# Masked softmax: the masks of the last two batches are moved among the divides on VectorE

## Chip, cores and metric

One core of a Trainium2 chip. The metric is the device time of the kernel in microseconds. The profile's times count from the start of its span, which is about 1.6 us shorter than the device time (155.0 against 156.66 in the profiled execution of the kernel before).

## The reference

```python
batch, heads, seq_q, seq_k = 16, 8, 256, 256
for b in range(batch):
    length = lengths[b]                      # 128 to 255, drawn per batch
    masked = x[b, :, :, :length].copy()
    masked = masked - np.max(masked, axis=-1, keepdims=True)
    exp_masked = np.exp(masked)
    result[b, :, :, :length] = exp_masked / np.sum(exp_masked, axis=-1, keepdims=True)
# the rest of result is 0
```

A batch is 2048 rows of 256 float32, 2 MiB. Batches 0 to 3 are loaded whole; the later loads fetch only a rounded-up prefix of each row. Stores always write whole rows.

## The kernel before

VectorE masks a batch (`clip`: a minimum with a ramp that is hugely negative past the length), ScalarE takes the exponentials with their row sums half a batch at a time, VectorE divides half a batch at a time, and SyncE stores. GpSimd issues the loads from batch 4 on. Batch b sits in slot b % 8; each of the 128 partitions holds `nt` = 16 of its rows (`half` is 8, `quarter` 4), and `ahead` is 4. Cuts are marked.

```python
def parts(b):                       # the pieces in which batch b is stored
    if b == 0:
        cuts = [0, nt]
    elif b < 8:
        cuts = [0, half, half + quarter, nt]
    elif b < 13 or b == batch - 1:
        cuts = [0, half, nt]
    else:
        cuts = [0, nt]              # 13 and 14: whole
    return [slice(i, j) for i, j in zip(cuts, cuts[1:])]
# ... (cut)
# SyncE
for b in range(batch):
    s_b = s_st[b % 2]
    for s in parts(b):
        nc.sync.wait_ge(s_out, 2 * b + (s.stop - 1) // half + 1)      # L117: the divides
        if b >= 2 and s.start == 0:
            nc.sync.wait_ge(s_b, 64 * (b // 2 + 1))                   # L119: store b-2 landed
        nc.sync.dma_start(out=out_f[b, :, s, :], in_=xt[:, b % slots, s, :]
                          ).then_inc(s_b, 16 * ((s.stop - s.start) // quarter))   # L120
for par in range(2):
    nc.sync.wait_ge(s_st[par], 64 * (batch // 2 + 1))                 # L124: all stores landed
# ... (cut)
# VectorE
def divide(b, h):
    s = slice(h * half, (h + 1) * half)
    nc.vector.wait_ge(s_exp, 2 * b + h + 1)
    step(nc.vector.reciprocal(out=inv_sum[:, b, s], in_=row_sum[:, b, s]))        # L221
    nc.vector.wait_ge(s_v, v)
    t = xt[:, b % slots, s, :]
    nc.vector.tensor_tensor(out=t, in0=t,
        in1=inv_sum[:, b, s, None].to_broadcast([P, half, seq_k]), op=ALU.mult
    ).then_inc(s_out, 1)                                                          # L224

mask(0, slice(0, half))
mask(0, slice(half, nt))
for b in range(batch):
    first = b == 0 or b >= ahead
    if first:
        divide(b, 0)
    if b + 1 < batch:
        mask(b + 1, slice(0, nt))
    if not first:
        divide(b, 0)
    divide(b, 1)
# ScalarE waits for s_min (the masks) and counts s_exp up by one for each half batch
```

The softmax here doesn't subtract the row's maximum and nothing guards it: scores larger than these inputs give would overflow.

## Time and profile before

| | kernel before |
|---|---|
| device time, median of 3 | 156.42 us (156.28 to 156.44) |
| VectorE, ScalarE busy | 75%, 68% of the span |
| traffic | 62.08 MB, mean 401 GB/s |
| load of batch 15 lands | 134.97 us |
| store of batch 14 issued | 141.10 us |
| last divide ends | 147.94 us |
| last packet of the last store | 152.99 us |

The last row is from the trace's single packet records: each store comes with sixteen records of 4 bytes, which I take for the ends of the parts of the 16 transfer engines, and I use the start of the last of these. The records don't name the engine.

Two of the page's rows of groups give VectorE's durations. Columns: line, engine, operation, operands and count; then busy us and the mean ns of one; then idle us ahead of them and what ended it.

```profile
L224 DVE TENSOR_TENSOR xt<-xt,inv_sum 128x2048 f32<-128x2048 f32 x32 | 73.3, 2292 | 1.1
L197 DVE SCALAR_TENSOR_TENSOR xt<-down,len_s,xt 128x2048 f32<-128x2048 f32 (+1 forms) x17 | 37.8, 2223 | 14.3 <-DMA xt<-in_x_dram 14.2
```

A multiply takes 2.29 us; the mask's mean of 2.22 mixes in two half-size ones of 1.28, a whole one takes 2.35.

### The profile page before, as it was taken

The numbers are of one execution on the slowest core, as the hardware profiler recorded it, in microseconds if no ns is written. First come the engines' busy times: TensorE is split into PE (matmuls) and PEld (weight loads), VectorE is DVE, ScalarE is ACT, GpSimd is POOL, SyncE is SP. The second block draws the span as 40 slices with busy tenths as digits, with TensorE's granted clock in tenths as the row PEclk, the third lists the DMA queues.
The fourth block names the chain that finished last, engine by engine and source line by source line (L and its number), as shares of the span: only waits on it lengthen the run. The fifth ranks groups of instructions, "written<-read, shape, count | busy, mean of one in ns | idle before, by whom it ended". The sixth has DMA issues, their size and how long they took to land.

```text
span 155.0 us, 1317 instructions
## 1 busy us (share of the span) xinstructions
PE 0.2 (0%) x1; PEld 0.1 (0%) x1; DVE 115.8 (75%) x84; ACT 105.2 (68%) x514; POOL 19.0 (12%) x25
## 2 busy tenths in 40 slices
PE   0000000000000000000000000000000000000000
PEld 0000000000000000000000000000000000000000
DVE  1339999953999696969889696969669619696810
ACT  3097799992692959688795939596973933959500
POOL 4910031000220200200211020202001000000000
DMA  4999999999999999999999999999999999999992
GB/s 110 427 457 410 440 376 422 401 408 440 412 409 392 403 410 420 409 415 414 407 422 406 419 405 411 415 412 424 410 420 412 428 439 427 412 450 423 395 425 85
DMA packets 9988, 62.08 MB, mean 401 GB/s; under 512 B 850, under 2 KB 946, under 8 KB 6274
## 3 DMA queue, kind: packets, MB, share of 16 engines
q1 hardware_dynamic: 5904, 41.95, 65.8%
q0 software_dynamic: 4080, 20.12, 32.0%
q14 instruction: 2, 0.02, 0.0%
q10 hardware_dynamic: 2, 0.00, 0.0%
HBM read 28.51 MB, written 33.55 MB: 400 GB/s over the span
## 4 chain that ended last, share of the span: by engine, by line
DMA 74%; DVE 6%; issue 6%; ACT 4%; POOLq 2%; SPq 1%; ACTq 1%; DVEq 0%
DMA xt<-in_x_dram 65%; DMA out_dram<-xt 10%; ACT xt L254 4%; DVE xt L197 3%; DVE xt L224 3%; ACTq L254 1%; SPq L109 1%; POOLq L132 0%; POOLq L137 0%; SPq L120 0%; POOLq L99 0%; DVE inv_sum L221 0%; SPq L111 0%; POOLq L159 0%; POOLq L155 0%
## 5 line engine op out<-in xcount | busy, mean ns | idle before, releaser
L254 ACT ACTIVATE xt<-xt x256 | 102.4, 402 | 38.6 <-DVE xt L197 38.6
L224 DVE TENSOR_TENSOR xt<-xt,inv_sum 128x2048 f32<-128x2048 f32 x32 | 73.3, 2292 | 1.1
L197 DVE SCALAR_TENSOR_TENSOR xt<-down,len_s,xt 128x2048 f32<-128x2048 f32 (+1 forms) x17 | 37.8, 2223 | 14.3 <-DMA xt<-in_x_dram 14.2
L254 ACT ACTIVATION_READ_ACCUMULATOR xt<-xt x256 | 48.1, 188 | 0.0
L132 POOL DMA_DIRECT2D xt<-in_x_dram x12 | 12.8, 1064 | 96.8 <-issue 57.4
L221 DVE RECIPROCAL inv_sum<-row_sum 128x8 f32<-128x8 f32 x32 | 6.4, 199 | 14.4 <-ACT xt L254 14.4
L151 POOL MEMSET xt<- 128x1536 f32 x4 | 5.3, 1387 | 1.1 <-DVE len_s L188 1.1
L246 ACT ACT_TABLE_LOAD x1 | 1.3, 1283 | 1.6 <-SPq L79 1.6
L180 DVE TENSOR_SCALAR down<-iota_i 128x256 f32<-128x256 int32 x1 | 0.3, 298 | 1.6 <-POOL iota_i L143 1.6
L185 DVE CAST len_b<-word 1x16 bf16<-1x16 int32 x1 | 0.2, 161 | 0.4 <-DMA word<-in_lengths_dram 0.4
L188 DVE TENSOR_SCALAR len_s<-len_f 128x16 f32<-128x16 f32 x1 | 0.2, 174 | 0.3 <-PE len_f L167 0.3
L143 POOL IOTA iota_i<- 128x256 int32 x1 | 0.3, 331 | 0.6 <-SPq L79 0.6
L148 POOL MEMSET seed<- 1x1 f32 x2 | 0.3, 162 | 0.0
L246 ACT ACTIVATE warm<-const-float32-0.0 128x1 f32<-128x1 f32 x1 | 0.2, 203 | 0.0
L146 POOL MEMSET ones<- 1x128 bf16 x1 | 0.2, 196 | 0.0
L167 PE MATMUL len_f<-len_b,ones 1*128 1x16 bf16 x1 | 0.2, 164 | 2.6 <-DVE len_b L185 2.6
L272 POOL MEMSET const-float32-0.0<- 128x1 f32 x1 | 0.1, 99 | 0.3 <-issue 0.3
L167 PEld LDWEIGHTS len_f<-len_b,ones 1*128 1x128 bf16 x1 | 0.1, 99 | 2.6 <-POOL ones L146 2.6
L272 POOL MEMSET const-float32-1.0<- 128x1 f32 x1 | 0.1, 99 | 0.0
L272 POOL MEMSET const-bfloat16-1.0<- 128x1 bf16 x1 | 0.1, 99 | 0.0
L272 POOL MEMSET const-uint8-127<- 128x1 uint8 x1 | 0.1, 99 | 0.0
L272 POOL BASE_LOAD x1 | 0.0, 17 | 0.1
## 6 DMA issues: line engine op xcount, KB each, us to landing
out_dram<-xt SPq DMA_DIRECT2D x19, 1024.0 KB
out_dram<-xt SPq DMA_DIRECT2D x14, 512.0 KB
xt<-in_x_dram SPq DMA_DIRECT2D x3, 2048.0 KB, 16.0
out_dram<-xt SPq DMA_DIRECT2D x3, 2048.0 KB
xt<-in_x_dram POOLq DMA_DIRECT2D x3, 1728.0 KB, 17.8
xt<-in_x_dram POOLq DMA_DIRECT2D x2, 2048.0 KB, 18.5
xt<-in_x_dram POOLq DMA_DIRECT2D x2, 1600.0 KB, 17.3
xt<-in_x_dram POOLq DMA_DIRECT2D x2, 1280.0 KB, 15.0
```

Of the source, the lines that this page charges most:

```text
L109: nc.sync.dma_start(out=xt[:, 0, s], in_=x_f[0, :, s]).then_inc(s_ld[h], 16)
L132: nc.gpsimd.dma_start(out=xt[:, slot, :, :w], in_=x_n[:, n, :, :w]).then_inc(s_sw[par], 16)
L143: nc.gpsimd.iota(iota_i, pattern=[[1, seq_k]], base=0, channel_multiplier=0).then_inc(s_iota, 1)
L148: nc.gpsimd.memset(seed[:, par : par + 1], 0.0).then_inc(s_st[par], 64)
L151: nc.gpsimd.memset(xt[:, b, :, low:], 0.0).then_inc(s_fill, 1)
L167: nc.tensor.matmul(len_f, lhsT=ones, rhs=len_b, start=True, stop=True).then_inc(s_lenf, 1)
L197: return nc.vector.scalar_tensor_tensor(out=t, in0=down[:, None, lo:hi].to_broadcast([P, s.stop - s.start, hi - lo]), scalar=len_s[:, b : ...
L221: step(nc.vector.reciprocal(out=inv_sum[:, b, s], in_=row_sum[:, b, s]))
L224: nc.vector.tensor_tensor(out=t, in0=t, in1=inv_sum[:, b, s, None].to_broadcast([P, half, seq_k]), op=ALU.mult,).then_inc(s_out, 1)
L246: nc.scalar.activation(out=warm, in_=nc.const_aps.tensor(0.0, (P, 1), F32), func=EXP)
L254: ins = nc.scalar.activation(out=e, in_=e, func=EXP, accum_out=sum_h[:, bass.ds(i, 1), j])
L272: nc = _bacc.Bacc("TRN2", target_bir_lowering=False, num_devices=1)
```

## The change

The intent is to have VectorE do in the last stretch what is ready: the divides of batch 13 need not stand behind the wait for batch 14's load, and the last mask, which starts the last exponentials, goes as early as it can.

```diff
-            first = b == 0 or b >= ahead
-            if first:
-                divide(b, 0)
-            if b + 1 < batch:
-                mask(b + 1, slice(0, nt))
-            if not first:
-                divide(b, 0)
-            divide(b, 1)
+            at = 0 if b == batch - 2 else 2 if b == batch - 3 else 1 if b == 0 or b >= ahead else 0
+            for h in range(3):
+                if h == at and b + 1 < batch:
+                    mask(b + 1, slice(0, nt))
+                if h < 2:
+                    divide(b, h)
```

`at` is the number of a batch's two divides that go ahead of the next batch's mask: now both for batch 13 and none for batch 14. For all other batches the order is the same as before.

## The prediction

> **What bounds the kernel now.** I read the page's forty slices first. The row of transfer engines stands at 9 from the second slice to the last but one, and the rate stays at 375 to 457 GB/s; VectorE is busy 75% and ScalarE 68% of the span.
>
> ```profile
> DMA  4999999999999999999999999999999999999992
> GB/s 110 427 457 410 440 376 422 401 408 440 412 409 392 403 410 420 409 415 414 407 422 406 419 405 411 415 412 424 410 420 412 428 439 427 412 450 423 395 425 85
> ```
>
> So the kernel is bound by its traffic (62.08 MB), and a reordering on VectorE can gain only where it fills a hole in that row, and can lose only where it makes one. The page's chain agrees in the large, but it needs care at its end:
>
> ```profile
> DMA 74%; DVE 6%; issue 6%; ACT 4%; POOLq 2%; SPq 1%; ACTq 1%; DVEq 0%
> ```
>
> It is followed back from the last compute instruction, not from the last byte. The last compute instruction is the last divide (ends 147.94); the span is 155.0, and SyncE waits for the final stores in between. I therefore read the last 30 us twice, as VectorE sees them and as the stores see them. VectorE's timeline:
>
> ```profile
> 122.35 2.29 DVE L224 TENSOR_TENSOR xt<-xt,inv_sum 128x2048 f32<-128x2048 f32 x1
> ...
> 127.91 2.35 DVE L197 SCALAR_TENSOR_TENSOR xt<-down,len_s,xt 128x2048 f32<-128x2048 f32 x1 [3.27 <-DMA xt<-in_x_dram]
> 130.18 0.20 DVE L221 RECIPROCAL inv_sum<-row_sum 128x8 f32<-128x8 f32 x1
> 130.41 2.29 DVE L224 TENSOR_TENSOR xt<-xt,inv_sum 128x2048 f32<-128x2048 f32 x1
> ...
> 133.85 0.20 DVE L221 RECIPROCAL inv_sum<-row_sum 128x8 f32<-128x8 f32 x1 [1.15 <-ACT xt L254]
> 134.09 2.29 DVE L224 TENSOR_TENSOR xt<-xt,inv_sum 128x2048 f32<-128x2048 f32 x1
> ...
> 136.29 2.34 DVE L197 SCALAR_TENSOR_TENSOR xt<-down,len_s,xt 128x2048 f32<-128x2048 f32 x1
> ...
> 138.78 2.29 DVE L224 TENSOR_TENSOR xt<-xt,inv_sum 128x2048 f32<-128x2048 f32 x1
> ...
> 142.46 2.29 DVE L224 TENSOR_TENSOR xt<-xt,inv_sum 128x2048 f32<-128x2048 f32 x1
> ...
> 145.65 2.29 DVE L224 TENSOR_TENSOR xt<-xt,inv_sum 128x2048 f32<-128x2048 f32 x1
> ```
>
> L197 is a mask, L221 with L224 a divide of half a batch. In order: first divide of batch 13, mask 14, second divide of 13, first divide of 14, mask 15, second divide of 14, the two divides of 15. Mask 14 waits 3.27 us for its load, while the exponentials of 13 are all done by 125.27 (ScalarE's timeline): the second divide of 13 stands behind a wait that isn't its own.
>
> The stores' side, from SyncE's timeline, SyncE's waits (124 to 134.2, then the whole run) and the windows of the end:
>
> ```profile
> 133.81 0.37 SPq L120 DMA_DIRECT2D out_dram<-xt  x1
> 141.10 0.36 SPq L120 DMA_DIRECT2D out_dram<-xt  x1
> ```
> ```profile
> SPq L119 <- DMA out_dram<-xt: 10.3, 1, 10.3
> ...
> SPq L124 <- DMA out_dram<-xt: 5.1, 1, 5.1
> ```
> ```profile
> 135.00:141.00 6.00, 0.00 (x0) 0.00 (x0) 5.97 (x4) 4.12 (x22) 0.00 (x0) 1.00 1.04 444
> 141.00:143.00 2.00, 0.00 (x0) 0.00 (x0) 0.82 (x3) 2.00 (x11) 0.00 (x0) 1.00 0.89 377
> 143.00:151.50 8.50, 0.00 (x0) 0.00 (x0) 4.25 (x3) 2.38 (x12) 0.00 (x0) 1.00 0.99 417
> 151.50:153.50 2.00, 0.00 (x0) 0.00 (x0) 0.00 (x0) 0.00 (x0) 0.00 (x0) 1.00 0.23 94
> ```
>
> Batches 13 and 14 are stored whole, in one transfer each after both divides. Store 13 goes out at 133.81 although its second divide ended at 132.70: SyncE stood 10.3 us at L119, for store 11 to land. Store 14 goes out at 141.10, right after its second divide (138.78 + 2.29 = 141.07). The windows' last two columns are the DMA share and GB/s: full to 141, a small hole between 141 and 143, full again, then a thin tail.
>
> **What the skill says.** (1) The Trainium skill, "DMA: Bandwidth & Descriptors", Queues, rings and completion order: each of the 16 engines has its own ring per queue and consumes descriptors in ring order. The trace fits: the trace's single packet records show 13 engines finishing store 13 between 141.5 and 142.2 and three at 142.9 to 143.2; in the last store the same 13 end at 151.9 to 152.0, and three at 152.6 to 153.0. (2) The same page, Anatomy of one DMA: transfer engines do not wait on semaphores; the issuing sequencer does. So a late divide delays the issue, and the ring runs dry. (3) The same page, Latency and other measured facts: about 600 ns to the first byte for transfers issued by SyncE. Here store 14, issued at 141.10, has its first packets at 141.92, so I use 0.82 us. (4) "VectorE: DVE Perf Modes", Mode 1x: one result per cycle at 0.96 GHz, so 2048 elements take 2.13 us as an estimate; the trace has 2.29 for a divide and 2.35 for a mask, which I use.
>
> **The change part by part.** The comparison of instruction order on each engine shows the same 156 rows on VectorE; nothing is added or removed and all other engines keep their order. Two things move.
>
> *Mask 14 behind both divides of 13.* The second divide of 13 can start when ScalarE is done (125.27): reciprocal 125.30, multiply 125.54 to 127.83. Back to back the next instruction starts some 2.2 us after a multiply's start (134.09 to 136.29) and 2.27 after a mask's (127.91 to 130.18), so VectorE is free at about 127.8. Mask 14 started at 127.91, set by its load, and will again: cost 0. Gain: the second divide of 13 ends 4.9 us earlier (132.70 to 127.8), but store 13 still waits at L119 for store 11 until 133.8, and behind that queues in rings that still hold store 12 (packet records: until about 138). Gain for the stores: 0.
>
> *Mask 15 ahead of both divides of 14.* Load 15 lands at 134.97 (issue 117.41 plus 17.56 in the chain). A mask that waits for a load starts 0.23 later (115.94 to 116.17 for mask 13), so mask 15 starts at 135.2 instead of 136.29: 1.1 us earlier. But VectorE now idles from 130.2 to 135.2, and leaves the first divide of 14, ready at 133.85, undone. Then, with 2.27 for a mask to the next start, and 0.23 + 2.21 = 2.44 for a divide: first divide of 14 from 137.5, second from 139.9, multiply 140.15 to 142.44. Store 14 is issued at 142.47 instead of 141.10: **1.37 us later** (2.44 for the divide moved behind, less 1.1 for the earlier mask). The divides of 15: from 142.4, end 144.9 (144.75 before), and from 144.8, end 147.3 (147.94 before). So the last store's issue is 0.6 us earlier, the next to last 0.1 later.
>
> *What this makes of the end.* Store 14 would have its first packets at 142.47 + 0.82 = 143.29. The 13 early engines ran dry at 141.5 to 142.2 and began again at about 141.95; now they begin at 143.29, 1.34 later. From there they have a fixed queue (stores 14 and 15, 4.19 MB), 151.9 − 141.95 = 9.95 us of it, and end at 153.2 to 153.3. The three late engines run dry at 142.9 to 143.2, so they wait 0.1 to 0.4 us; the last of them ends at 152.99 + 0.13 = 153.1. Before, the end was set by that last engine at 152.99. So the finish moves by 153.25 − 152.99 = **0.2 to 0.3 us**: most of the 1.34 us is absorbed, since the engines that lose it had about 1.0 us to spare. The earlier last divide gains nothing: the stores of 15 queue behind store 14, until about 148.2.
>
> **The rivals.** (A) *The compute chain sets the end*: the last divide ends 0.6 us earlier, so 155.8. For it speaks that the chain ends in L224; against it, that the last store's issue at 147.97 meets rings that are full until 149.4. (B) *The whole delay of store 14 is paid*: plus 1.3 us, 157.8. This is so if the three late engines are late only in the profiled execution, or if they are late by their rate and wait too. I can't tell from one trace; the bounds are 0.1 for their own wait and 1.34. (C) *The earlier divide of 13 brings its store forward and closes the hole*: at most the hole, 0.11 × 2 = 0.2 us, so 156.2. Against: L119 and store 12. (D) *The order of loads changes*, a gain or a loss in the queue of reads: the last load is issued at 117.41, before the first moved instruction, so nothing.
>
> **Range and chances.** My sum gives 156.42 + 0.25, and I add a little for (B), which I hold at a quarter: 156.7. From (C) to most of (B): 156.3 to 157.6. Two per cent is 3.1 us; no path I see reaches it either way, as the hole can't exceed the 1.4 us of issue delay.
>
> **What would show it.** In the changed profile: mask 14 at 127.9 with no shorter wait for the load, store 13 still at about 133.8; mask 15 at about 135.2 after some 5 us of idle; store 14 issued at about 142.5; the window 141 to 143 falling from a share of 0.89 to about 0.5; the thin tail after 151.5 becoming a fuller one with nearly the same end. The prediction is wrong if store 13's earlier issue changes the share of reads against writes, if store 14 goes out no later, or if the tail keeps its three stragglers and the end moves by the whole 1.3 us.

## The result

| | before | after |
|---|---|---|
| device time, median of 4 | 156.43 us (156.28 to 156.60) | 156.46 us (156.19 to 156.51) |
| load of batch 15 lands | 134.97 | 134.55 |
| mask 15 starts | 136.29 | 134.79 |
| store 13, store 14 issued | 133.81, 141.10 | 133.91, 142.04 |
| last divide ends | 147.94 | 146.89 |
| last packet: the engines from first to last | 151.86 to 152.99 | 152.79 to 152.97 |

The ratio after/before is 0.9998, 95% interval 0.9981 to 1.0016: the same. Here and below a ratio is the mean time of one kernel's fast runs over that of the other's in the same rounds, so it isn't quite the ratio of the medians quoted.

VectorE's timeline of the changed kernel (start us, duration us, engine, line, operation, operands, count, then idle before it and what ended that):

```profile
124.88 0.20 DVE L221 RECIPROCAL inv_sum<-row_sum 128x8 f32<-128x8 f32 x1 [0.66 <-ACT xt L253]
125.11 2.29 DVE L224 TENSOR_TENSOR xt<-xt,inv_sum 128x2048 f32<-128x2048 f32 x1
127.46 2.35 DVE L197 SCALAR_TENSOR_TENSOR xt<-down,len_s,xt 128x2048 f32<-128x2048 f32 x1
134.79 2.35 DVE L197 SCALAR_TENSOR_TENSOR xt<-down,len_s,xt 128x2048 f32<-128x2048 f32 x1 [4.98 <-DMA xt<-in_x_dram]
...
137.28 2.29 DVE L224 TENSOR_TENSOR xt<-xt,inv_sum 128x2048 f32<-128x2048 f32 x1
...
139.72 2.29 DVE L224 TENSOR_TENSOR xt<-xt,inv_sum 128x2048 f32<-128x2048 f32 x1
...
142.16 2.29 DVE L224 TENSOR_TENSOR xt<-xt,inv_sum 128x2048 f32<-128x2048 f32 x1
...
144.60 2.29 DVE L224 TENSOR_TENSOR xt<-xt,inv_sum 128x2048 f32<-128x2048 f32 x1
```

The second divide of batch 13 now runs ahead of mask 14 without a long wait. The 3.27 us of idle ahead of mask 14 are gone, and 4.98 us of idle ahead of mask 15 have come in their place. Both divides of batch 14 stand behind it, and the second ends at 142.01.

SyncE's timeline and waits of the changed kernel, as shown of the one before:

```profile
133.91 0.36 SPq L120 DMA_DIRECT2D out_dram<-xt  x1
142.04 0.37 SPq L120 DMA_DIRECT2D out_dram<-xt  x1
```
```profile
SPq L119 <- DMA out_dram<-xt: 10.0, 1, 10.0
...
SPq L124 <- DMA out_dram<-xt: 6.0, 1, 6.0
```

Store 13 hasn't moved, though its divides ended 5 us earlier: L119, the wait for store 11, still holds SyncE for 10.0 us. The final wait grew from 5.1 to 6.0 us, because the last issue is earlier and the landing is not.

The windows of the end (length in us; busy us and count of PE, weight loads, VectorE, ScalarE, GpSimd; granted clock; DMA share; GB/s), and the page's row of transfer engines. The view counts a packet wholly in the window in which it starts, so a share can exceed 1:

```profile
135.00:141.00 6.00, 0.00 (x0) 0.00 (x0) 5.93 (x5) 5.16 (x27) 0.00 (x0) 1.00 1.03 441
141.00:143.00 2.00, 0.00 (x0) 0.00 (x0) 1.97 (x3) 2.00 (x12) 0.00 (x0) 1.00 0.60 254
143.00:151.50 8.50, 0.00 (x0) 0.00 (x0) 3.86 (x3) 0.88 (x5) 0.00 (x0) 1.00 0.97 409
151.50:153.50 2.00, 0.00 (x0) 0.00 (x0) 0.00 (x0) 0.00 (x0) 0.00 (x0) 1.00 0.63 262
```
```profile
DMA  4999999999999999999999999999999999997994
```

The hole between 141 and 143 has deepened from a share of 0.89 to 0.60, and the tail after 151.5 has filled from 0.23 to 0.63. What was lost in the hole came back in the tail: before, thirteen engines finished at 151.9 to 152.0 and three at 152.6 to 153.0; after, all sixteen finish between 152.79 and 152.97.

The page's chain of work, shares of the span by engine:

```profile
DMA 75%; DVE 12%; issue 4%; POOLq 2%; SPq 1%; DVEq 0%
```

ScalarE has left the chain (4% before) and VectorE's share has doubled: from the landing of load 15 on, mask 15 and four divides follow one another without a gap. The chain's last instruction ends 1.05 us earlier (147.94 to 146.89), and the time did not follow.

### The profile page after: what moved, and what is told of

It is laid out like the page before. It is cut to its first block, busy times and chain, and to the rows that moved or that the text cites. A ratio compares the mean times of both kernels' runs of the same rounds, so it can differ in the third digit from the quotient of the medians.

```text
span 154.9 us, 1317 instructions
## 1 busy us (share of the span) xinstructions
PE 0.2 (0%) x1; PEld 0.1 (0%) x1; DVE 115.7 (75%) x84; ACT 105.2 (68%) x514; POOL 19.0 (12%) x25
## 4 chain that ended last, share of the span: by engine, by line
DMA 75%; DVE 12%; issue 4%; POOLq 2%; SPq 1%; DVEq 0%
DMA xt<-in_x_dram 64%; DMA out_dram<-xt 11%; DVE xt L224 9%; DVE xt L197 3%; SPq L109 1%; POOLq L137 0%; DVE inv_sum L221 0%; POOLq L132 0%; SPq L120 0%; POOLq L99 0%; SPq L111 0%; POOLq L159 0%; POOLq L155 0%; DVEq L214 0%; POOLq L161 0%
```

## The experiments

My theory: the end is the later of two things, three transfer engines that run late whatever VectorE does, and the issue of store 14 plus the time that its bytes and those of store 15 need. The change moves the second up to the first. Rivals: the two halves of the change gain and lose equal amounts; the last divide sets the end; the whole delay of store 14 is paid; SyncE's wait at L119 hides a gain.

### The first half alone (e1_mask14_only)

```diff
-            at = 0 if b == batch - 2 else 2 if b == batch - 3 else 1 if b == 0 or b >= ahead else 0
+            at = 2 if b == batch - 3 else 1 if b == 0 or b >= ahead else 0
```

> The first half of the change alone: mask 14 behind both divides of batch 13, mask 15 where it was. My theory: nothing moves for the stores. Mask 14 at about 127.9 (its load), the second divide of 13 done by 127.8 but store 13 still issued at about 133.8, store 14 at about 141.1, DMA share of 0.89 between 141 and 143, time 156.4 (ratio 0.998 to 1.002). Rival, two effects that cancel in the changed kernel: this half gains what the other loses, so this run is faster, 155.4 to 156.0.

Measured: 156.45 us, ratio 1.000 (0.998 to 1.002). Store 13 was issued at 133.73, store 14 at 140.65. The gain of the rival is absent. Load 15 landed at 134.54 in the profiled execution, and store 14 came early enough that there was no hole (share 1.02 between 141 and 143).

### The second half alone (e2_mask15_only)

```diff
-            at = 0 if b == batch - 2 else 2 if b == batch - 3 else 1 if b == 0 or b >= ahead else 0
+            at = 0 if b == batch - 2 else 1 if b == 0 or b >= ahead else 0
```

> The second half alone: mask 15 ahead of both divides of batch 14, mask 14 where it was. My theory: as the whole change. Store 14 about 1 to 1.4 us later (142.0 to 142.5), DMA share between 141 and 143 at about 0.6, the tail after 151.5 at about 0.63 instead of 0.23, time 156.4 to 156.7 (ratio 1.000 to 1.002). Rival, two effects that cancel: slower by 0.4 to 1.0 us, 156.8 to 157.4.

Measured: 156.60 us, ratio 1.0013 (0.9992 to 1.0034). The time is as expected, the profile isn't: store 14 went out at 140.93 and the hole had a share of 0.91. In this execution load 15 landed at 133.43, 1.1 us earlier than in the changed kernel's. Over all profiled executions it landed between 133.0 and 135.0 (the full-width run aside), while the first engine always ended store 13 at 141.3 to 141.6. The edits of e3, e4, e5, e6, e7 and e9 act only after load 15 has landed, and these runs with the kernel before cover 133.03 to 134.97, so there the edit doesn't explain the spread. So how much of a hole store 14 leaves differs from execution to execution, and single profiles have to be compared by the issue of store 14, not by the kernel's name. Neither half moves the time by a resolved amount. By the intervals e1 gains at most 0.3 us and e2 loses at most 0.5, so the two halves could cancel by 0.3 us at most.

### Store 14 held a little, compute untouched (e3_store14_exp31)

```diff
                 nc.sync.wait_ge(s_out, 2 * b + (s.stop - 1) // half + 1)
+                if b == batch - 2:
+                    nc.sync.wait_ge(s_exp, 2 * b + 3)
```

> The kernel before, with one wait more on SyncE: store 14 waits for the exponentials of the first half of batch 15 (done at 142.1). No compute instruction moves. My theory (thirteen engines have about 1.0 us to spare on three): store 14 at about 142.2, 1.1 us later, hole of 0.6 between 141 and 143, time 156.4 to 156.6 (ratio 1.000 to 1.002). Rival (the whole delay is paid, and in the changed kernel the earlier last divide pays it back): 157.3 to 157.5. Rival (the last divide sets the end): 156.4, so this run alone does not tell the last two points of my theory apart from it; the run that delays the last divide does.

Measured: 156.38 us, ratio 1.0001 (0.9982 to 1.0020). The profile is inconclusive: load 15 landed at 133.03, so even with the added wait store 14 left at 140.29, and no hole opened.

### The last divide held (e4_last_divide_late)

```diff
             nc.vector.wait_ge(s_v, v)
+            if (b, h) == (batch - 1, 1):
+                twice = down[:, None, :].to_broadcast([P, 4, seq_k])
+                nc.vector.tensor_tensor(out=idle, in0=twice, in1=twice, op=ALU.add)
             t = xt[:, b % slots, s, :]
```

> The kernel before with 1.2 us of idle work on VectorE (an addition of 128x1024 into a tile that nobody reads) just ahead of the last multiply. Rival (the last divide sets the end, as the chain has it): the whole 1.2 us is paid, 157.6 (ratio 1.007). My theory: the last store's issue moves from 148.0 to 149.1, its first packets to 149.95, some 0.5 us after thirteen engines run dry (149.4), and these have about 1.0 us to spare on the three late ones: 156.4 to 156.5 (ratio 1.000 to 1.001).

Measured: 156.39 us, ratio 1.0001 (0.9982 to 1.0020). The added work is there in VectorE's timeline, on the path of the last divide (line numbers shift with the inserted lines):

```profile
144.64 0.20 DVE L222 RECIPROCAL inv_sum<-row_sum 128x8 f32<-128x8 f32 x1 [0.66 <-ACT xt L258]
144.88 1.22 DVE L226 TENSOR_TENSOR idle<-down 128x1024 f32<-128x1024 f32 x1
146.02 2.28 DVE L228 TENSOR_TENSOR xt<-xt,inv_sum 128x2048 f32<-128x2048 f32 x1
```

The last store left at 148.33, not at the expected 149.1, because load 15 had landed earlier (134.21) than in the first profile. The added 1.22 us (1.14 to the multiply's start) cost nothing that the runs resolve. The upper end of the interval, 0.3 us, excludes the 1.2 that the chain of work would have it cost. So the last divide doesn't set the end, and I don't expect the changed kernel's earlier last divide to have gained.

### Store 14 held by VectorE (e5_store14_dummy)

The same insertion, for `(b, h) == (batch - 2, 1)` and with 8 rows instead of 4 (2.3 us).

> The kernel before with 2.3 us of idle work on VectorE just ahead of the second multiply of batch 14, about double the delay of the changed kernel: store 14 at about 143.4 instead of 141.1, the last divide only some 0.3 us later since VectorE waited there before. My theory: thirteen engines start store 14 at about 144.2 and end about 154.2, 1.2 us after the three late ones used to end: 157.6 (157.2 to 157.9). Whole delay paid: 158.7. Last divide sets the end: 156.7.

Measured: 156.69 us against 156.23 before, ratio 1.0023 (1.0006 to 1.0040): 0.36 us by the ratio, not 1.2. The expectation took the landing of load 15 from the first profile (134.97); here it was 133.78, and store 14 went out at 142.12 instead of 143.4. From that issue on it behaves as expected: all engines end between 152.88 and 153.03. The time is the one that the rival of the last divide gave (156.7), but that divide ended at 146.96, 1 us earlier than in the kernel before, so it doesn't explain the time. And e7 below, in the same rounds, has a shift of the same size without a cause that I know, so nothing here rests on the 0.36 us.

### Store 14 held longer, compute untouched (e6_store14_out31)

```diff
+                if b == batch - 2:
+                    nc.sync.wait_ge(s_out, 2 * b + 3)
```

> The kernel before, with one wait more on SyncE: store 14 waits for the first divide of batch 15 (144.75), so it goes out at about 144.8, 3.7 us later, and no compute instruction moves. My theory: the end moves by 3.7 less the 1.0 us to spare, 2.6 to 2.7 us: 159.1 (158.7 to 159.4). Whole delay paid: 160.1. Last divide sets the end: 156.4.

Measured: 158.68 us against 156.23, ratio 1.0149 (1.0118 to 1.0181): 2.3 us by the ratio, a little under the expected 2.6 and just under the range's lower end of 158.7. Its timed runs spread from 157.5 to 159.4, where those of the kernel before spread over 0.6 us. That would fit an end that hangs on store 14's issue, which follows load 15; only one of the executions was traced. In the profiled execution store 14 left at 143.33. The windows show the hole reach past 141 to 143 and the tail full:

```profile
141.00:143.00 2.00, 0.00 (x0) 0.00 (x0) 2.00 (x1) 2.00 (x12) 0.00 (x0) 1.00 0.39 164
151.50:153.50 2.00, 0.00 (x0) 0.00 (x0) 0.00 (x0) 0.00 (x0) 0.00 (x0) 1.00 1.00 414
```

### Store 14 in halves (e7_store14_halves)

```diff
-        elif b < 13 or b == batch - 1:
+        elif b < 13 or b >= batch - 2:
```

> The kernel before, with batch 14 stored in two halves, each after its divide, so that the first goes out at about 136.5 (or once store 12 has landed) and the rings never run dry at 142. My theory: the hole between 141 and 143 closes (share 0.89 to about 1.0), thirteen engines end some 0.4 us earlier, and the end, set by the three late ones, does not move: 156.4 (ratio 0.999 to 1.001). Rival (every hole in the traffic counts): 156.2 (ratio 0.9985).

Measured: 156.63 us against 156.23, ratio 1.0021 (1.0006 to 1.0036). The first half went out at 138.72 and the packet records show no hole between 141 and 143. Thirteen engines end at 151.3 to 151.95, earlier than before, the last three at 152.20, 152.57 and 152.93. (The windows view has a share of 0.90 there, since it counts each packet by its start; summed by overlap, the records give 1.01 here, 0.92 before the change and 0.54 after it.) So closing the hole gains nothing, as expected. The 0.3 us by which the timed runs are slower was not expected, and the profiled execution doesn't show where it lies (its last packet is at 152.93, before's at 152.99). The edit also makes two transfers of one, which this run doesn't separate. That stays open.

### Store 13 without SyncE's wait (e8_store13_no_wait)

On the changed kernel:

```diff
-                if b >= 2 and s.start == 0:
+                if b >= 2 and s.start == 0 and b != batch - 3:
```

> The changed kernel without SyncE's wait ahead of store 13 for store 11 to land, so that the earlier second divide of batch 13 can bring its store forward: from 133.9 to about 127.5. My theory: it only queues sooner behind store 12 in the same rings, the load of batch 15 lands at the same 134.6 to 135.0, and the end does not move: 156.4 (ratio 0.998 to 1.002). Rival (SyncE's wait hid the gain): faster by up to the hole that store 14 leaves, 155.6 to 156.1.

Measured: 156.46 us against 156.23, ratio 1.0012 (0.9997 to 1.0027). SyncE's timeline:

```profile
127.61 0.36 SPq L120 DMA_DIRECT2D out_dram<-xt  x1
...
142.23 0.37 SPq L120 DMA_DIRECT2D out_dram<-xt  x1
```

Store 13 now leaves 6 us earlier, and the end doesn't move: load 15 lands at 134.74 and the first engine ends store 13 at 141.4, as in all the runs. The earlier store did take a little from the reads: between 128 and 133 they moved 1.31 MB, against 1.41 in the changed kernel and 1.43 in the one before. Load 15 was not later by more than its usual spread. The wait at L119 hid no gain.

### Store 14 held to the last divide (e9_store14_out32)

```diff
+                if b == batch - 2:
+                    nc.sync.wait_ge(s_out, 2 * batch)
```

> The kernel before, with store 14 held on SyncE until the last divide (146.0 to 148.0, depending on when load 15 lands in the execution). From the runs so far I take a law: the last packet ends at the later of 152.6 to 153.0 (the three late engines) and the issue of store 14 plus 10.93. Law: for an issue at 147.0 the last packet ends at 157.9, five us later than before, time 161.4 (160.4 to 162.4), slower by over 2%; the law is wrong if issue to last packet is not within 0.1 of 10.93. Last divide sets the end: 156.4.

Measured: 162.40 us against 156.31, ratio 1.0395 (1.0369 to 1.0420). SyncE's timeline and the windows:

```profile
147.77 0.36 SPq L122 DMA_DIRECT2D out_dram<-xt  x1
```
```profile
144.00:147.00 3.00, 0.00 (x0) 0.00 (x0) 2.30 (x3) 1.14 (x6) 0.00 (x0) 1.00 0.00 0
```

The transfer engines stand still from 144 to 147, and the last packet is at 158.69, 10.92 after the issue. The law held at its far end; the time is at the upper end of its range because store 14 left at 147.77 and not at 147.0. With the profiled executions in order of store 14's issue:

| kernel | load 15 lands | store 14 issued | store 13's last packet | last packet | after the issue | after store 13's last |
|---|---|---|---|---|---|---|
| e3 | 133.03 | 140.29 | 142.85 | 152.66 | 12.37 | 9.81 |
| e4 | 134.21 | 140.33 | 142.72 | 152.54 | 12.21 | 9.82 |
| e1 | 134.54 | 140.65 | 142.96 | 152.78 | 12.13 | 9.82 |
| e2 | 133.43 | 140.93 | 143.10 | 152.88 | 11.95 | 9.78 |
| before | 134.97 | 141.10 | 143.16 | 152.99 | 11.89 | 9.83 |
| after | 134.55 | 142.04 | 143.20 | 152.97 | 10.93 | 9.77 |
| e5 | 133.78 | 142.12 | 142.74 | 153.03 | 10.91 | 10.29 |
| e8 | 134.74 | 142.23 | 142.84 | 153.16 | 10.93 | 10.32 |
| e6 | 133.57 | 143.33 | 143.01 | 154.26 | 10.93 | 11.25 |
| e9 | 134.79 | 147.77 | 144.06 | 158.69 | 10.92 | 14.63 |

Up to about 141.9 the end doesn't depend on the issue and lies at 152.5 to 153.0: it comes 9.8 us after the last engine has ended store 13. (In these rows it also rises with the issue, but e7, whose first half left at 138.72, ended at 152.93, again 9.81 after store 13's last packet at 143.12.) From there on it is the issue plus 10.9. The bend is where the late engines' 152.5 to 153.0 less 10.9 puts it: 141.6 to 142.1. The changed kernel sits on it: both columns fit.

The records also say what "late" means. In the kernel before, the gap between the thirteenth engine and the first late one is 0.69 us at the end of store 13 and 0.60 at the end of store 15, so the late ones don't run slower there; they carry a lag. In e9, where all sixteen stand still and begin store 14 together, they end within 0.16 us of one another (158.53 to 158.69). What the hole takes from the thirteen is a lead that is worth nothing.

### Full-width loads (e10_full_width)

```diff
-                pick(v_len, bass.ds(n, 1), bass.ds(n % slots, 1), par, widths + [seq_k])
+                pick(v_len, bass.ds(n, 1), bass.ds(n % slots, 1), par, [seq_k])
```

> The kernel before with every load of batches 4 to 15 at the full 256 columns (5.0 MB more to read, so some 12 us longer, about 168). It asks where the lag of three engines comes from. If from the short rows of the narrow loads: the 16 engines end within 0.3 us of one another. If it is there whatever the rows are: three of them still end 0.5 to 1.1 us after the rest.

Measured in a single run, its state unknown: 167.14 us, where about 168 was expected. The engines end the last store between 160.56 and 162.88, the last four at 161.45, 161.82, 162.62 and 162.88. That is neither of the two expected pictures: two engines are clearly late, the third by 0.37 us only. Late engines are there without narrow rows, so narrow rows aren't their only cause. What is stays open.

## Why the prediction was right

- *Mask 14 moved costs and gains nothing*: right. Mask 14 started at 127.46 with its load (127.22), not behind the divide. Store 13 stayed at 133.9, and with the wait at L119 taken away (e8) its 6 us gained nothing either.
- *Mask 15 starts 1.1 us earlier, store 14 leaves 1.37 later*: right in its steps. In the profile of after, mask 15 starts 0.24 after its load (0.23 was used), then 2.27 and twice 2.44 follow. The issue was at 142.04 instead of 142.47, only because load 15 landed 0.42 us earlier in that execution (134.55 against 134.97). I had taken one execution's landing for fixed; over the profiled executions it varies by 2 us. In the profiles with mask 15 ahead of both divides (after, e2, e8) store 14 left 7.5 us after the landing, so landings of 133.0 to 135.0 put it at 140.5 to 142.5. The 142.47 that I used was thus near the latest, and in an execution like e2 (140.93) there is hardly a delay to absorb. So the time stayed the same in part because the loads landed earlier than I had assumed; that part is luck.
- *The hole deepens and the tail absorbs it*: right. The share between 141 and 143 was 0.60 where I wrote about 0.5, and the tail filled to 0.63. The end of the packets was 152.97 in the profiled execution, where I had 153.25; with the landing 0.42 earlier, 152.83 is what my sum would have given. The predicted loss of 0.2 to 0.3 us is not resolved: the interval of the ratio reaches from a gain of 0.30 us to a loss of 0.25. Two slips in the working don't change it: 2.44 less 1.1 is 1.34 and not 1.37, and engines that ended store 13 as late as 142.16 can't have begun again at 141.95. That the same thirteen engines are early in both stores was assumed, since the records have no names.
- *Rival A (the last divide sets the end)*: refuted by e4 and e6; delaying that divide by 1.1 us cost nothing that the runs resolve, and holding a store with the divide untouched cost 2.3 us.
- *Rival B (the whole delay is paid)*: refuted below the bend and right above it. The timed runs exclude its 1.3 us, but by the landings above many of them will have had a smaller delay, so the slack itself rests on the profiles: after, with the issue 0.94 us later and the end 0.02 earlier, and the two columns of the table under e9. Its second ground, that the three engines are late by their rate, is refuted by the lag that doesn't grow.
- *Rivals C and D*: e8 shows no gain from an earlier store 13 and e7 none from a closed hole; the loads landed in the same range with either order, and the reads between 128 and 133 moved 1.43 MB before and 1.41 after, so the sign of being wrong that I had named did not come.

None of the versions beat the kernel before. The intent failed on two counts: the work that mask 14's wait held back was wanted by no one yet, and the work that mask 15's wait now holds back, the first divide of 14, was the one that the queue of stores came to need.

## What to carry to other kernels

When the transfers bound a kernel, judge a reordering of compute by the moment at which a queue would run dry against the moment at which the next transfer is issued, and not by the chain of work, which follows the last compute instruction. Put no wait for a load ahead of work that feeds a store about to be needed; e6 and e9 show what a store's late issue costs once the queue is dry. And where some transfer engines run behind the others, a small hole can be free on those in front: the tail of the last store shows how much (here about 1 us).

## What the Trainium skill lacked or had wrong

- "DMA: Bandwidth & Descriptors", Latency and other measured facts, has two of the sixteen engines (7 and 15) usually slower. Here the last store's packet records have three late ones, by 0.6 to 1.0 us after the next (152.02) in the kernel before and by 0.4 to 1.4 us after the next (161.45) in the full-width run; the records don't say which engines. The lag didn't grow over the last two stores, so there it isn't a lower rate. The page gives no size for the difference.
- The same section gives about 600 ns to the first byte for a transfer issued by SyncE, and doesn't say from which moment. With the queue dry (e5, e6, e8, e9) the first data packets of the sixteen engines started 0.84 to 0.99 us after SyncE's issuing instruction began; that instruction lasts 0.36 to 0.37 us, so 0.47 to 0.63 after it ended.
- I found no page with a measure for what a dry queue costs at the end. Here every microsecond by which store 14 was issued past about 141.9 moved the last packet by one (142.04 to 147.77 in, 152.97 to 158.69 out).
- I found no page that says how far a load's landing varies between executions. With the kernels' common loads it was 133.0 to 135.0 for batch 15, while the timed runs of the kernel before agree within 0.6%. It is the issue that varies (115.47 to 117.41 where the chain shows it); from there to the landing it took 17.56 to 17.72 us.
